# Half of the prompt heads' exponentials turned in 32x32 blocks on VectorE

## The chip, the cores and the metric

The kernel runs on one core of a Trainium2 chip. Its engines are TensorE (PE), VectorE (DVE), ScalarE (ACT), GpSimd (POOL) and SyncE (SP), which here issues the DMAs. The metric is the device time of one execution in microseconds; three runs of the kernel before took 2255.1, 2255.21 and 2255.36 us, a median of 2255.21 us.

## The reference

Two layers of an encoder trunk over two groups of tokens: a prompt of 1024 positions and a sample of 256. Each layer adds to x the normalised output projection of four gated branches (attention, a Fourier mix, spatial gating, attention into memory). The change is in the attention branch: eight query heads of 64, two key/value heads (heads 0 to 3 read key/value head 0, heads 4 to 7 read 1), no mask.

```python
def self_attention(q, k, v):
    ...
    def one_block(qblk):
        s = jnp.einsum('bqkgd,bskd->bkgqs', qblk, k, preferred_element_type=jnp.float32) * scale
        p = jax.nn.softmax(s, axis=-1)
        return jnp.einsum('bkgqs,bskd->bqkgd', p.astype(v.dtype), v)
...
    o_att = self_attention(q, k, v) * jax.nn.silu(ag)
```

All of it is float32. The kernel writes many operands as a sum of a high and a low part in the type f32r, and multiplies the parts.

## The kernel before

The work of a layer comes in the order spatial gating, Fourier, memory attention, the attention's projections, attention, output projection. Attention goes over ten tiles of 128 queries, t = 0 to 7 of the prompt (1024 keys) and 8, 9 of the sample (256 keys); tile by tile over eight heads h; kv = h // 4 is the key/value head and j = h % 4 the place within it.

For one head of a prompt tile: `score` (L742) makes 128 x 1024 scores in PSUM with four matmuls of 512 columns (L752), DVE takes the negated row maximum (L755), ACT the exponential with its row sum (L757). `turn` (L760) transposes the 128 x 1024 exponentials on PE, eight blocks of 128 x 128 (L770), through two PSUM buffers; ACT copies the first half to SBUF (L773), DVE the second (L775). The copies are `pt[kv]`, keys on partitions. `values` (L788) takes one block of 128 keys (kt) at a time for all four heads of each kv: two matmuls of 512 columns onto the two halves of PSUM's partitions (L796); after the last block DVE multiplies by the gate (L801) and SP stores four pieces (L803).

`norm_gate` (L777) turns the reciprocal row sums: a reciprocal (L780) and a broadcast to 128 x 512 (L782) on DVE, four transposes on PE (L785), a product into the gate on DVE (L786). `prep_q` (L713) loads a tile's queries and splits them: high part on ACT (L143), low part on DVE (L144). `turn_q` (L720) transposes them on PE (L724) and copies on ACT (L726) and DVE (L728).

The main loop (L815) sets the order on PE: in the step of head h come the scores of the next head, then one piece of `todo` (the norm and values of the tile before), at h = 4 and 5 a `turn_q` for the next tile, then the turn of h. The block is emitted under `manual_schedule` for PE, so PE runs in this order; on the other engines a scheduler that simulates the timeline decides the order when the program is built. Every engine works through its own list in order. In tile 0 the loop also emits one attention gate (`attention_gates`, L620) every second head, and in tiles 8 and 9 one output product a head (`product`, L871).

## Time and profile before

| | |
|---|---|
| runs | 2255.1, 2255.21, 2255.36 us |
| profiled execution, span from first to last instruction | 2254.6 us |
| PE busy | 2208.9 us, 98% |
| DVE busy | 1167.4 us, 52% |
| ACT busy | 844.2 us, 37% |
| POOL busy | 206.3 us, 9% |
| mean granted TensorE clock | 0.996 |

The profiled execution took its span of 2254.6 us, 0.6 us under the median of the runs. Attention's tiles lie at about 727 to 975 us in layer 0 and 1791 to 2040 us in layer 1. Busy shares are means over the whole span; a group of instructions by line shows its busy time, the mean of one and what the engine waited for before it. A timeline gives start and duration; where like instructions follow each other they are one row with a count, and rows of PE overlap, as matmuls are pipelined. A step is the distance between two starts.

### The profile page before, as it was taken

What the parts mean: (1) busy time and instruction counts of PE and PEld (TensorE: products, weight loads), DVE (VectorE), ACT (ScalarE), POOL (GpSimd) and SP (SyncE); (2) the same over time, 40 slices, a digit from 0 to 9 for tenths busy, and PEclk for the clock granted to TensorE, in tenths of its full rate; (3) what the DMA queues carried; (4) which work ended last, traced back from release to release, by engine and by line L of the source; (5) the groups of instructions that cost most, each with busy time, mean ns of one, the idle gap of its engine ahead of it and who ended that gap; (6) DMA issues with size and microseconds to landing.
All of it is one profiled execution on the core that took longest, in us unless ns stands there. A gap on an engine that the chain in (4) does not pass through costs nothing.

```text
span 2254.6 us, 32607 instructions
## 1 busy us (share of the span) xinstructions
PE 2208.9 (98%) x12872; PEld 1837.5 (82%) x12872; DVE 1167.4 (52%) x2096; ACT 844.2 (37%) x1915; POOL 206.3 (9%) x376
## 2 busy tenths in 40 slices
PE   7999999999999999999999999999999999999997
PEld 7898988888998655578888988888899865567885
DVE  5345344545573777634465344445467377753445
ACT  6133332334332655541254222234342255554121
POOL 2010000000140000000062000000014000000005
PEclk9999999999999999999999999999999999999998
DMA  4123321201122210222343121020112221123234
GB/s 171 59 96 132 128 93 59 99 31 55 58 76 75 66 34 29 84 80 92 112 142 109 57 75 59 33 99 31 59 54 81 78 64 29 31 83 99 88 109 140
DMA packets 96200, 177.31 MB, mean 79 GB/s; under 512 B 12208, under 2 KB 47408, under 8 KB 96048
## 3 DMA queue, kind: packets, MB, share of 16 engines
q1 hardware_dynamic: 96048, 175.23, 23.1%
q8 instruction: 101, 1.65, 0.3%
q14 instruction: 51, 0.42, 0.1%
HBM read 129.05 MB, written 46.14 MB: 78 GB/s over the span
## 4 chain that ended last, share of the span: by engine, by line
PE 90%; ACT 2%; DMA 2%; DVE 2%; POOL 2%; issue 1%; SPq 0%; DVEq 0%; POOLq 0%; ACTq 0%
PE mm L248 34%; PE mm L877 16%; PE mm L261 12%; PE mm L796 6%; PE mm L770 6%; PE s L752 5%; PE mm L311 2%; PE mm L327 1%; PE s L422 1%; PE s L408 1%; PE s L576 1%; PE mm L609 1%; POOL c L902 1%; PE s L217 1%; DMA wr<-in_w_in_dram 1%
## 5 line engine op out<-in xcount | busy, mean ns | idle before, releaser
L248 PE MATMUL mm<-a,ws 128*128 128x512 f32 (+1 forms) x4032 | 795.4, 355 | 0.0
L248 PEld LDWEIGHTS mm<-a,ws 128*128 128x128 f32 x4032 | 663.9, 189 | 102.3 <-issue 0.5
L877 PE MATMUL mm<-ws,a 128*128 128x512 f32 x1632 | 380.5, 391 | 0.0
L877 PEld LDWEIGHTS mm<-ws,a 128*128 128x128 f32 x1632 | 303.9, 188 | 63.7 <-issue 1.6
L261 PE MATMUL mm<-ws,a 128*128 128x256 f32 x2400 | 302.7, 287 | 0.0
L261 PEld LDWEIGHTS mm<-ws,a 128*128 128x128 f32 x2400 | 295.6, 194 | 0.5 <-DVE a L234 0.2
L757 ACT ACTIVATE c<-s,st 128x1024 f32<-128x1024 f32 (+1 forms) x160 | 158.1, 988 | 154.8 <-DVE st L755 153.9
L755 DVE TENSOR_REDUCE st<-s 128x1 f32<-128x1024 f32 (+1 forms) x160 | 170.2, 1064 | 73.1 <-PE s L752 71.0
L770 PEld LDWEIGHTS mm<-ident,c 128*128 128x128 f32 x1088 | 117.1, 141 | 90.1 <-issue 26.0
L273 ACT ACTIVATE c<-mm 128x512 f32<-128x512 f32 (+1 forms) x96 | 50.7, 528 | 342.1 <-PE mm L248 338.3
L274 DVE SCALAR_TENSOR_TENSOR c<-c,mm 128x512 f32<-128x512 f32 (+1 forms) x96 | 57.3, 597 | 231.3 <-ACT c L273 231.3
L752 PE MATMUL s<-c,c 128*128 128x512 f32 (+1 forms) x576 | 162.6, 399 | 1.1 <-ACT c L726 1.1
L770 PE MATMUL mm<-ident,c 128*128 128x128 f32 x1088 | 151.8, 279 | 5.0 <-ACT c L757 5.0
L796 PE MATMUL mm<-a,c 128*64 128x512 f32 x512 | 140.2, 618 | 2.7 <-ACT a L773 2.7
L902 POOL TENSOR_TENSOR c<-c,c 128x512 f32<-128x512 f32 x40 | 56.1, 1401 | 891.5 <-ACT c L897 891.4
L166 ACT ACTIVATE ws<-wr,pre_g 128x256 fp32r<-128x256 f32 x304 | 126.6, 505 | 22.6 <-DMA wr<-in_w_in_dram 16.5
L167 DVE SCALAR_TENSOR_TENSOR ws<-wr,pre_g,ws 128x256 fp32r<-128x256 f32 x304 | 128.7, 484 | 2.2 <-ACT ws L166 2.0
L886 DVE TENSOR_TENSOR c<-c,mm 128x512 f32<-128x512 f32 x120 | 81.1, 682 | 85.1 <-PE mm L877 85.1
L775 DVE COPY a<-mm 128x512 f32<-128x512 f32 x128 | 88.3, 690 | 66.3 <-PE mm L770 66.1
L752 PEld LDWEIGHTS s<-c,c 128*128 128x128 f32 x576 | 98.5, 189 | 14.9 <-ACT c L726 1.3
L150 POOL TENSOR_TENSOR st<-st,mhalf 128x1 f32<-128x1 f32 (+3 forms) x120 | 99.7, 831 | 9.9
L148 POOL TENSOR_SCALAR st<-st 128x1 f32<-128x1 f32 (+3 forms) x120 | 27.2, 227 | 744.2 <-DVE st L654 455.5
(119 smaller groups left out, 2133.9 us busy)
## 6 DMA issues: line engine op xcount, KB each, us to landing
wr<-in_w_in_dram SPq DMA_DIRECT2D x76, 512.0 KB, 4.0
wr<-in_w_out_dram SPq DMA_DIRECT2D x32, 512.0 KB, 4.5
wr<-o SPq DMA_DIRECT2D x64, 256.0 KB, 2.9
c<-in_x_prompt_dram SPq DMA_DIRECT2D x16, 512.0 KB, 6.1
o<-c SPq DMA_DIRECT2D x32, 256.0 KB, 2.0
wr<-in_w_mem_kv_dram SPq DMA_DIRECT2D x16, 512.0 KB, 4.4
q<-c SPq DMA_DIRECT2D x40, 128.0 KB, 1.7
ag<-c SPq DMA_DIRECT2D x80, 64.0 KB, 1.6
```

Of the source, the lines that this page charges most:

```text
L150: nc.gpsimd.tensor_tensor(r, m, mhalf[:, :n], ALU.pow)
L166: nc.scalar.activation(w[:, 0, kk], raw[:, k], AF.Copy, scale=g)
L167: nc.vector.scalar_tensor_tensor(w[:, 1, kk], raw[:, k], g, fv(w)[:, 0, kk], ALU.mult, ALU.subtract)
L248: nc.tensor.matmul(acc[:, :n], w[:, a, k, c * P:(c + 1) * P], hT.t[g][b][:, k, :], start=i == 0, stop=i == 3 * KC - 1)
L261: nc.tensor.matmul(acc[:, :256], hT.t[g][a][:, k, tt * P:(tt + 1) * P], w[:, b, k, :], start=i == 0, stop=i == 3 * KC - 1)
L752: nc.tensor.matmul(s[:, c0:c0 + n], e["qT"][:, h, :], kT[kg][b][:, kv, :], start=b == 0, stop=b == 1)
L755: nc.vector.tensor_reduce(nm, s[:, :nk], axis=AX.X, op=ALU.max, negate=True)
L757: nc.scalar.activation(p[:, :nk], s[:, :nk], AF.Exp, bias=nm, accum_out=e["rs"][:, j, kv:kv + 1])
L770: nc.tensor.transpose(pt[:, kk, :], p[:, c0:c0 + P], ident)
L775: nc.vector.tensor_copy(dst, pt[:, :kn])
L796: nc.tensor.matmul(acc[kv * HD:(kv + 1) * HD].rearrange("p j t -> p (j t)"), vt, e["pt"][kv][:, kt].rearrange("p j t -> p (j t)"), start=k ...
L877: nc.tensor.matmul(acc, oT[g][c][:, a, tt * P:(tt + 1) * P], w[:, b, c, :], start=j == 0, stop=j == 11)
```

## The change

For the heads with j of 2 or 3 in prompt tiles, the turn leaves PE. DVE turns the exponentials in blocks of 32 x 32 within each 32 partitions (L778 of the new kernel) into a buffer `blocks`, and after j = 3 SP issues 16 DMAs (L784), each of 32 partitions by 2 KB, which put block (a, b) into the place (b, a) of a buffer `pd`. So there are 32 such DMAs a tile. Heads with j of 0 and 1 stay on PE; both of their copies are now on ACT (L798). The heads of a prompt tile come in the order 2, 0, 3, 1, 6, 4, 7, 5.

`values` now works on two parts, j of 0 and 1 from `pt` and j of 2 and 3 from `pd`; a matmul has 256 columns instead of 512, and a piece of `todo` has two blocks of keys (L831). The columns of the second part are read in runs of 32. The broadcast of the reciprocals goes to POOL (L805), and `norm_gate` is one step later than before. The query split is on ACT (L726) and POOL (L727), the raw queries are loaded one tile earlier, and both query copies are on ACT (L734). The attention gates keep their number and size but change their order, so that those within tile 0 are of 512 columns. Comments and docstrings elsewhere are removed.

```diff
     def attention_gates(l, hT, ag):
         w = {}
-        for i, g in ((0, 0), (0, 1), (1, 0), (1, 1), (0, 2), (1, 2)):
+        for i, g in ((0, 0), (1, 0), (0, 2), (1, 2), (0, 1), (1, 1)):
...
     def attention(l, q_d, kT, v8, v2, ag, o_d):
+        raw = {}
+        def load_q(t):
+            if t < NT:
+                raw[t] = c2([P, 8, HD])
+                nc.sync.dma_start(raw[t], q_d[t])
         def prep_q(t):
-            q = c2([P, 8, HD])
-            nc.sync.dma_start(q, q_d[t])
+            q = raw.pop(t)
             qhl = c4([P, 8, 2, HD], F32R)
-            split(qhl[:, :, 0, :], qhl[:, :, 1, :], q)
+            nc.scalar.copy(qhl[:, :, 0, :], q)
+            nc.gpsimd.tensor_tensor(qhl[:, :, 1, :], q, fv(qhl)[:, :, 0, :], ALU.subtract)
             return qhl
-        def turn_q(qhl, qT, kvs):
-            for kv in kvs:
-                pt = mm([P, 4, P], F32R)
-                for j in range(4):
-                    nc.tensor.transpose(pt[:, j, :], qhl[:, 4 * kv + j].rearrange("p a d -> p (a d)"), ident_r)
-                if kv == 0:
-                    nc.scalar.copy(qT[:, 0:4], fv(pt))
-                else:
-                    nc.vector.tensor_copy(qT[:, 4:8], fv(pt))
+        def turn_q(qhl, qT, kv):
+            pt = mm([P, 4, P], F32R)
+            for j in range(4):
+                nc.tensor.transpose(pt[:, j, :], qhl[:, 4 * kv + j].rearrange("p a d -> p (a d)"), ident_r)
+            nc.scalar.copy(qT[:, 4 * kv:4 * kv + 4], fv(pt))
         tiles = {}
         def open_tile(t):
-            g, _ = group_of(t)
-            nk = SEQ if g < 2 else DEC
-            gt = c2([P, 4, P])
-            nc.sync.dma_start(gt, ag[t])
-            alloc = a16 if g < 2 else c4
-            tiles[t].update(
-                nk=nk, gt=gt, rs=st([P, 4, 2], tag="rowsum", bufs=3),
-                pt=[alloc([P, nk // P, 4, P], F32) for _ in range(2)])
+            e = dict(prompt=t < 8, nk=SEQ if t < 8 else DEC, qT=c4([P, 8, P], F32R),
+                     rs=st([P, 4, 2], tag="rowsum", bufs=3))
+            tiles[t] = e
+        def open_rest(t):
+            e = tiles[t]
+            e["gt"] = c2([P, 4, P])
+            nc.sync.dma_start(e["gt"], ag[t])
+            if e["prompt"]:
+                e["pt"] = a16([P, 8, 2, 2, P], F32)
+                e["pd"] = a16([P, 4, 2, 8, 2, 32], F32)
+            else:
+                e["pt"] = [c4([P, 2, 4, P]) for _ in range(2)]
         def score(t, h):
             g, _ = group_of(t)
@@ -759,87 +770,121 @@
         def turn(t, h):
             e = tiles[t]
-            nkt = e["nk"] // P
             kv, j = h // 4, h % 4
             p = e.pop(h)
-            for half in range((nkt + 3) // 4):
-                kn = min(4, nkt)
+            if e["prompt"] and j >= 2:
+                if j == 2:
+                    e["blocks"] = a8([P, 4, 8, 2, 32], F32)
+                nc.vector.transpose(e["blocks"][:, :, :, j - 2].rearrange("p b k q -> p k b q"),
+                                    p.rearrange("p (k b q) -> p k b q", b=4, q=32))
+                if j == 3:
+                    for r in range(4):
+                        for a in range(4):
+                            b = (a + r) % 4
+                            nc.sync.dma_start(
+                                e["pd"][32 * b:32 * b + 32, a, kv].rearrange("p k j q -> p (k j q)"),
+                                e["blocks"][32 * a:32 * a + 32, b].rearrange("p k j q -> p (k j q)"))
+                return
+            for half in range(2 if e["prompt"] else 1):
+                kn = 4 if e["prompt"] else 2
                 pt = mm([P, 4, P])
                 for kk in range(kn):
                     c0 = (half * 4 + kk) * P
                     nc.tensor.transpose(pt[:, kk, :], p[:, c0:c0 + P], ident)
-                dst = e["pt"][kv][:, half * 4:half * 4 + kn, j, :]
-                if half == 0:
-                    nc.scalar.copy(dst, pt[:, :kn])
+                if e["prompt"]:
+                    dst = e["pt"][:, half * 4:half * 4 + kn, kv, j, :]
                 else:
-                    nc.vector.tensor_copy(dst, pt[:, :kn])
-
-        def norm_gate(t):
+                    dst = e["pt"][kv][:, :, j, :]
+                nc.scalar.copy(dst, pt[:, :kn])
+        def norm_rows(t):
             e = tiles[t]
             r = st([P, 4, 2], tag="rowsum_r", bufs=2)
             nc.vector.reciprocal(r, e["rs"])
-            rb = c2([P, 4, 2, HD])
-            nc.vector.tensor_copy(rb, r.unsqueeze(3).to_broadcast([P, 4, 2, HD]))
+            e["rb"] = c2([P, 4, 2, HD])
+            nc.gpsimd.tensor_copy(e["rb"], r.unsqueeze(3).to_broadcast([P, 4, 2, HD]))
+        def norm_gate(t):
+            e = tiles[t]
             rt = mm([P, 4, P])
             for j in range(4):
-                nc.tensor.transpose(rt[:, j, :], rb[:, j].rearrange("p a d -> p (a d)"), ident)
+                nc.tensor.transpose(rt[:, j, :], e["rb"][:, j].rearrange("p a d -> p (a d)"), ident)
             nc.vector.tensor_tensor(e["gt"], e["gt"], rt, ALU.mult)
-        def values(t, kt):
+        def values(t, part, kts):
             e = tiles[t]
-            nkt = e["nk"] // P
-            if kt == 0:
+            if "acc" not in e:
                 e["acc"] = mm([P, 4, P])
             acc = e["acc"]
-            for kv in range(2):
-                vt = (v8 if t < 8 else v2)[:, kt, kv * HD:(kv + 1) * HD]
-                nc.tensor.matmul(acc[kv * HD:(kv + 1) * HD].rearrange("p j t -> p (j t)"), vt,
-                                 e["pt"][kv][:, kt].rearrange("p j t -> p (j t)"),
-                                 start=kt == 0, stop=kt == nkt - 1)
-            if kt == nkt - 1:
-                o = c2([P, 4, P])
-                nc.vector.tensor_tensor(o, acc, e["gt"], ALU.mult)
-                for j in range(4):
-                    nc.sync.dma_start(o_d[j][:, t * P:(t + 1) * P], o[:, j, :])
-                del tiles[t]
-
+            last = e["nk"] // P - 1
+            for kt in kts:
+                for kv in range(2):
+                    out = acc[kv * HD:(kv + 1) * HD]
+                    vt = (v8 if t < 8 else v2)[:, kt, kv * HD:(kv + 1) * HD]
+                    if not e["prompt"]:
+                        out, src = out.rearrange("p j t -> p (j t)"), e["pt"][kv][:, kt].rearrange("p j t -> p (j t)")
+                    elif part == 0:
+                        out, src = out[:, 0:2].rearrange("p j t -> p (j t)"), e["pt"][:, kt, kv].rearrange("p j t -> p (j t)")
+                    else:
+                        out = out[:, 2:4].rearrange("p j (a q) -> p j a q", q=32)
+                        src = e["pd"][:, :, kv, kt].rearrange("p a j q -> p j a q")
+                    nc.tensor.matmul(out, vt, src, start=kt == 0, stop=kt == last)
+        def finish(t):
+            e = tiles.pop(t)
+            o = c2([P, 4, P])
+            nc.vector.tensor_tensor(o, e["acc"], e["gt"], ALU.mult)
+            for j in range(4):
+                nc.sync.dma_start(o_d[j][:, t * P:(t + 1) * P], o[:, j, :])
+        load_q(0)
+        load_q(1)
         qhl = prep_q(0)
         yield
-        tiles[0] = dict(qT=c4([P, 8, P], F32R))
-        turn_q(qhl, tiles[0]["qT"], (0, 1))
         open_tile(0)
-        score(0, 0)
+        for kv in range(2):
+            turn_q(qhl, tiles[0]["qT"], kv)
+        open_rest(0)
+        order = {True: (2, 0, 3, 1, 6, 4, 7, 5), False: tuple(range(8))}
+        work = [(t, i, h) for t in range(NT) for i, h in enumerate(order[t < 8])]
+        score(0, work[0][2])
         yield
-        work = [(t, h) for t in range(NT) for h in range(8)]
         todo = []
-        for i, (t, h) in enumerate(work):
-            if h == 2 and t + 1 < NT:
+        for n, (t, i, h) in enumerate(work):
+            if i == 2 and t + 1 < NT:
                 qhl = prep_q(t + 1)
-            if h == 4 and t + 1 < NT:
-                tiles[t + 1] = dict(qT=c4([P, 8, P], F32R))
+            if i == 4 and t + 1 < NT:
+                load_q(t + 2)
                 open_tile(t + 1)
-            if i + 1 < len(work):
-                score(*work[i + 1])
+            if i == 7 and t + 1 < NT:
+                open_rest(t + 1)
+            if n + 1 < len(work):
+                score(work[n + 1][0], work[n + 1][2])
             if todo:
-                todo.pop(0)()
-            if h in (4, 5) and t + 1 < NT:
-                turn_q(qhl, tiles[t + 1]["qT"], (h - 4,))
+                for f in todo.pop(0):
+                    f()
+            if i in (4, 5) and t + 1 < NT:
+                turn_q(qhl, tiles[t + 1]["qT"], i - 4)
             turn(t, h)
-            if h == 7:
-                for f in todo:
-                    f()
-                todo = [lambda t=t: norm_gate(t)]
-                nkt = tiles[t]["nk"] // P
-                todo += [lambda t=t, kt=kt: values(t, kt) for kt in range(nkt)]
-                if nkt == 8:
-                    a, b = todo[0], todo[1]
-                    todo[0:2] = [lambda a=a, b=b: (a(), b())]
-            yield t, h
-        for f in todo:
-            f()
+            if i == 7:
+                for fs in todo:
+                    for f in fs:
+                        f()
+                norm_rows(t)
+                if t < 8:
+                    todo = [[lambda t=t, part=part, k=k: values(t, part, (k, k + 1))]
+                            for part in range(2) for k in range(0, 8, 2)]
+                    todo[1].append(lambda t=t: norm_gate(t))
+                else:
+                    todo = [[lambda t=t: norm_gate(t)]] + [[lambda t=t, k=k: values(t, 0, (k,))] for k in range(2)]
+                todo[-1].append(lambda t=t: finish(t))
+            yield t, i
+        for fs in todo:
+            for f in fs:
+                f()
```

PE, at the boundary of tiles 1 and 2 of layer 0: `s2_` are scores, `mm_` PSUM results, `a16_` the turned exponentials. Before, the steps of the first head of tile 2:

```order
L770 MATMUL mm_1039_7618<-ident_61,c4_1032_7585 128x128 x4
L770 MATMUL mm_1040_7624<-ident_61,c4_1032_7585 128x128 x4
L752 MATMUL s2_1041_7630<-c4_693_5346,c4_1013_7514 128x512
L752 MATMUL s2_1041_7630<-c4_694_5347,c4_1013_7514 128x512
L752 MATMUL s2_1041_7630<-c4_695_5348,c4_1013_7514 128x512
L752 MATMUL s2_1041_7630<-c4_696_5349,c4_1013_7514 128x512
L785 MATMUL mm_1046_7643<-ident_61,c2_1045_7641 128x128 x4
L796 MATMUL mm_1047_7649<-a16_961_7278,c4_698_5351 64x512
L796 MATMUL mm_1047_7649<-a16_962_7279,c4_698_5351 64x512
L770 MATMUL mm_1048_7652<-ident_61,c4_1037_7608 128x128 x4
L770 MATMUL mm_1049_7658<-ident_61,c4_1037_7608 128x128 x4
```

After, the second of tile 2's steps and the end of the first:

```order
L763 MATMUL s2_1032_7632<-c4_695_5348,c4_1005_7509 128x512
L763 MATMUL s2_1032_7632<-c4_696_5349,c4_1005_7509 128x512
L831 MATMUL mm_1035_7641<-a16_975_7375,c4_698_5351 64x256 x4
L763 MATMUL s2_1037_7648<-c4_693_5346,c4_1005_7509 128x512
L763 MATMUL s2_1037_7648<-c4_694_5347,c4_1005_7509 128x512
L763 MATMUL s2_1037_7648<-c4_695_5348,c4_1005_7509 128x512
L763 MATMUL s2_1037_7648<-c4_696_5349,c4_1005_7509 128x512
L831 MATMUL mm_1035_7641<-a16_975_7375,c4_698_5351 64x256 x4
L811 MATMUL mm_1040_7661<-ident_61,c2_1031_7630 128x128 x4
L793 MATMUL mm_1041_7667<-ident_61,c4_1034_7639 128x128 x4
L793 MATMUL mm_1042_7673<-ident_61,c4_1034_7639 128x128 x4
```

Before, every step has S (L752), V (L796) and T (L770). Now the step of head 2 has S and V only; the step of head 0 has S (here of head 3), V, N (L811) and T.

POOL in attention of layer 0. Before, its list goes from the key and query norms straight to the output's products (L902):

```order
L150 TENSOR_TENSOR st_890_6718<-st_889_6716,mhalf_65 128x4
L148 TENSOR_SCALAR st_894_6755<-st_893_6753 128x4
L150 TENSOR_TENSOR st_895_6757<-st_894_6755,mhalf_65 128x4
L902 TENSOR_TENSOR c4_1386_9063<-c4_1386_9063,c4_1580_10330 128x512
L902 TENSOR_TENSOR c4_1392_9091<-c4_1392_9091,c4_1580_10330 128x512
```

After, the low parts of the queries (L727, `c4_` of the tile) and the broadcasts (L805) stand in between; `c4_1043` are the queries of tile 3, `c2_1031` the broadcast for tile 1, and N above (`mm_1040`) reads `c2_1031`:

```order
L805 COPY c2_983_7400<-st_982_7398 128x512
L727 TENSOR_TENSOR c4_995_7449<-c2_955_7267,c4_995_7449 128x8x64
L727 TENSOR_TENSOR c4_1043_7679<-c2_1004_7507,c4_1043_7679 128x8x64
L805 COPY c2_1031_7630<-st_1030_7628 128x512
L805 COPY c2_1079_7860<-st_1078_7858 128x512
L727 TENSOR_TENSOR c4_1091_7909<-c2_1052_7737,c4_1091_7909 128x8x64
L727 TENSOR_TENSOR c4_1139_8139<-c2_1100_7967,c4_1139_8139 128x8x64
L805 COPY c2_1127_8090<-st_1126_8088 128x512
```

The broadcast for tile 1 stands behind the low part of tile 3's queries, which needs their high part. ACT makes that one (`c4_1043`, L726); its list after, in tile 2, `c4_1034` and `c4_1039` being the exponentials of heads 0 and 3:

```order
L798 COPY a16_975_7375<-mm_1028_7616 128x4x128
L798 COPY a16_975_7375<-mm_1029_7622 128x4x128
L768 ACTIVATE c4_1034_7639,st_1006_7510<-s2_1032_7632,st_1033_7637 128x1024
L768 ACTIVATE c4_1039_7655,st_1006_7510<-s2_1037_7648,st_1038_7653 128x1024
L726 CAST c4_1043_7679<-c2_1004_7507 128x8x64
L798 COPY a16_1022_7595<-mm_1041_7667 128x4x128
L798 COPY a16_1022_7595<-mm_1042_7673 128x4x128
```

The cast stands behind both exponentials. In the POOL list the same order returns two tiles on: L805, L805, L727, L727.

DVE in tile 2 of layer 0, after: `c4_1026`, `c4_1039` and `c4_1049` are the exponentials of heads 2, 3 and 6.

```order
L766 TENSOR_REDUCE st_1019_7568<-s2_1018_7563 128x1
L766 TENSOR_REDUCE st_1025_7602<-s2_1024_7597 128x1
L803 RECIPROCAL st_1030_7628<-st_957_7270 128x8
L766 TENSOR_REDUCE st_1033_7637<-s2_1032_7632 128x1
L778 STREAM_TRANSPOSE a8_1036_7646<-c4_1026_7604 128x8x4x32
L766 TENSOR_REDUCE st_1038_7653<-s2_1037_7648 128x1
L778 STREAM_TRANSPOSE a8_1036_7646<-c4_1039_7655 128x8x4x32
L836 TENSOR_TENSOR c2_1027_7610<-mm_987_7411,c2_925_7076 128x512
L812 TENSOR_TENSOR c2_974_7373<-c2_974_7373,mm_1040_7661 128x512
L766 TENSOR_REDUCE st_1045_7687<-s2_1044_7682 128x1
L766 TENSOR_REDUCE st_1048_7717<-s2_1047_7712 128x1
```

Before, a copy out of PSUM (L775) stood behind each reduce; now a transpose (L778) a pair of heads stands there, and the broadcast (L782) is gone. The product of tile 0 (L836) stands behind the transpose of head 3.

## Rows read from the trace of the kernel before

**Rows 1.** The page's busy shares; waits of PE: us, times, longest.

```profile
PE 2208.9 (98%) x12872; PEld 1837.5 (82%) x12872; DVE 1167.4 (52%) x2096; ACT 844.2 (37%) x1915; POOL 206.3 (9%) x376
...
PE mm L770 <- ACT c L757: 5.0, 8, 1.2
PE mm L796 <- ACT a L773: 2.7, 2, 1.4
```

**Rows 2.** Windows of two prompt tiles: span, engines' busy times, PEclk, DMA share, GB/s.

```profile
760.00:784.80 24.80, 24.80 (x142) 14.77 (x140) 18.15 (x23) 14.45 (x26) 0.00 (x0) 1.00 0.09 27
784.80:809.60 24.80, 24.80 (x142) 14.77 (x140) 18.15 (x23) 14.45 (x26) 0.00 (x0) 1.00 0.12 33
```

**Rows 3.** Timeline of PE in layer 0: start, duration, engine, line, operation.

```profile
811.12 1.17 PE L752 MATMUL s<-c,c 128*128 128x512 f32 x4
812.23 1.08 PE L796 MATMUL mm<-a,c 128*64 128x512 f32 x4
813.24 1.09 PE L770 MATMUL mm<-ident,c 128*128 128x128 f32 x8
814.08 1.17 PE L752 MATMUL s<-c,c 128*128 128x512 f32 x4
...
812.71 0.60 PE L796 MATMUL mm<-a,c 128*64 128x512 f32 x2
...
808.73 0.60 PE L785 MATMUL mm<-ident,c 128*128 128x128 f32 x4
809.26 0.65 PE L796 MATMUL mm<-a,c 128*64 128x512 f32 x2
...
822.12 0.54 PE L724 MATMUL mm<-ident_r,c 128*128 128x128 f32 x4
822.49 0.30 PE L770 MATMUL mm<-ident,c 128*128 128x128 f32 x1
```

**Rows 4.** Groups by line and shape: count, busy time, mean ns of one.

```profile
L902 POOL TENSOR_TENSOR c<-c,c 128x512 f32<-128x512 f32 x40 | 56.1, 1401 | 891.5 <-ACT c L897 891.4
L143 ACT CAST c<-c 128x512 fp32r<-128x512 f32 x28 | 17.5, 624 | 4.0 <-DVE c L491 4.0
L144 DVE TENSOR_TENSOR c<-c,c 128x512 fp32r<-128x512 f32 x28 | 19.1, 684 | 3.5 <-ACT c L143 3.5
L782 DVE COPY c<-st 128x512 f32<-128x512 f32 x20 | 8.4, 420 | 0.1
L726 ACT CAST c<-mm 128x512 fp32r<-128x512 f32 x20 | 11.6, 578 | 0.9 <-PE mm L724 0.9
L775 DVE COPY a<-mm 128x512 f32<-128x512 f32 x128 | 88.3, 690 | 66.3 <-PE mm L770 66.1
L773 ACT COPY a<-mm 128x512 f32<-128x512 f32 x128 | 74.2, 580 | 9.9 <-PE mm L770 9.9
```

**Rows 5.** Timeline of DVE and ACT there, and of a turn that waited.

```profile
812.33 1.22 DVE L755 TENSOR_REDUCE st<-s 128x1 f32<-128x1024 f32 x1 [0.24 <-PE s L752]
...
813.65 1.11 ACT L757 ACTIVATE c<-s,st 128x1024 f32<-128x1024 f32 x1 [1.72 <-DVE st L755]
814.76 0.58 ACT L773 COPY a<-mm 128x512 f32<-128x512 f32 x1
...
755.99 1.12 ACT L757 ACTIVATE c<-s,st 128x1024 f32<-128x1024 f32 x1
757.25 0.55 PE L770 MATMUL mm<-ident,c 128*128 128x128 f32 x3 [0.42 <-ACT c L757]
```

**Rows 6.** Timeline of PE: longest waits in tile 0 and sample tiles.

```profile
739.91 0.33 PE L770 MATMUL mm<-ident,c 128*128 128x128 f32 x1 [1.22 <-ACT c L757]
...
934.55 0.64 PE L796 MATMUL mm<-a,c 128*64 128x512 f32 x1 [1.36 <-ACT a L773]
```

**Rows 7.** SP's four stores of a tile; landing of one: KB, us.

```profile
882.26 1.75 SPq L803 DMA_DIRECT2D o<-c  x4
...
o<-c SPq DMA_DIRECT2D x80, 64.0 KB, 1.6
```

## The prediction

> **What bounds the kernel now.** I read the busy shares first: TensorE (PE) is busy for 98% of the span and next to nothing else is long [rows 1]. The waits of PE then say which of its rare gaps lie in attention: two lines there, 5.0 us before the turns (L770) and 2.7 us before the values (L796), over both layers [rows 1]. So attention is bound by what PE has to do, and the table by windows shows it: a prompt tile takes 24.80 us, all of it PE, with VectorE (DVE) at 18.15 us, ScalarE (ACT) at 14.45 us, GpSimd (POOL) at nothing and the clock at 1.00 [rows 2]. Last comes the timeline of one head. Its PE steps, start to start, are 1.11 us for scores (S), 1.01 us for values (V), 0.84 us for the eight turns (T): 2.96 us [rows 3]. A quarter turn of the queries (Q) adds 822.49 - 822.12 = 0.37 us, the norm's turn (N) 809.26 - 808.73 = 0.53 us [rows 3]. Per tile: 8 x 2.96 + 2 x 0.37 + 0.53 = 24.95 us, near the window's 24.80.
>
> **What goes.** In each of 16 prompt tiles (eight in each of two layers) four heads lose their turn on PE: 64 x 0.84 = -53.8 us.
>
> **What the split of the values adds.** V keeps its columns but cuts each matmul from 512 to 256. A V is now two pairs of passes (four records), and a pair takes 812.71 - 812.23 = 0.48 us [rows 3]. The same 512 columns of fp32 cost in T half of 0.84 = 0.42 us, so some 0.06 us of a pair does not scale with the columns. With four half pairs instead of two pairs, V grows by between 0 (it scales fully) and 2 x 0.06 = 0.12 us. I take 0.11 (the row's remainder, a little less for rounding): 128 x 0.11 = +14.1 us. The Trainium skill (TensorEngine Tiling (Array Packing), Instruction Overhead) puts some 60 cycles on a matmul, 0.025 us at 2.4 GHz as an estimate; by it the V term would be 128 x 0.05 = 6.4 instead of 14.1 us. The row shows more per pair, and I go by the row. PE's work so falls by 39.7 us, and a tile to about 22.4 us.
>
> **Does the chain through the DVE transpose keep up?** No row shows this instruction. The bounds for a block transpose of 128x1024 are 0.84 us (twice the 128x512 copy within SBUF, L782 [rows 4]) and 2.44 us (two passes at the rate of a 1024-element reduce, 1.22 us [rows 5]). I take one pass, 1.22 us, as for the reduce, which also touches every element once. In a pair of heads a (on DVE) and b (on PE), DVE runs reduce a, transpose a, reduce b in that order (only in the first pair of a tile reduce b comes ahead of transpose a). From the start of S(a): the reduce starts after 812.33 - 811.12 = 1.21, the exponential 1.32 later, at 2.53 [rows 3, 5]; a turn may follow an exponential's start after 757.25 - 755.99 = 1.26 [rows 5], at 3.79; the transpose holds DVE for 1.22, to 5.01; reduce b to exponential b 1.32, and 1.26 more: T(b) is possible at 7.59. PE gets there after three S, three V and one T: 3 x 1.11 + 3 x 1.12 + 0.84 = 7.53. It is a tie, so each tenth of a microsecond that the transpose takes beyond 1.22 shows; a wait at T(b) delays the next S(a) less than the next T(b), since that S was already issued, and I count half the excess. Where two query casts stand on ACT before the exponential of head 7, the tie breaks: S(7) at u; Q1 ends at u + 1.11 + 1.12 + 0.37 = 2.60, the cast [rows 4] holds ACT to about 3.2, transpose 7 starts 1.26 later at 4.46 and ends at 5.68, exponential 5 starts at 7.00, T(5) is possible at u + 8.26. PE has S, V, Q, T, S, V, S, V before it: 3 x 1.11 + 3 x 1.12 + 0.37 + 0.84 = 7.90. I take 0.35 in each of 16 tiles: +5.6 us.
>
> **The step that I think eats the gain: POOL's queue.** The broadcast of the reciprocal row sums (RB, L805) and the low half of the queries (lo, L727) are both on POOL now, and POOL works in order. For tiles 2, 4 and 6 the queue has the lo of the *next* tile ahead of the RB of the *previous* one. That lo needs the high half, which ACT casts (L726) behind the exponential of head 3; N, which needs RB, stands on PE at the second head of that tile, just behind S(3) and V. From the start of S(3): exponential 3 starts at 2.53, ACT is free 1.11 later (814.76 - 813.65) [rows 5], the cast takes 0.62, lo as a POOL tensor_tensor of 128x512 1.40 [rows 4]. RB has no row on POOL: between 0.42 (the copy on DVE that it replaces) and 1.40 (POOL's tensor_tensor), I take 0.9, the middle, as nothing says which row is nearer. Sum 2.53 + 1.11 + 0.62 + 1.40 + 0.90 = 6.56. PE arrives at 1.11 + 1.12 = 2.23. PE so waits 4.3 us, three times in each layer: 6 x 4.3 = +26.0 us. Bounds: lo at DVE's 0.68 [rows 4] and RB at 0.42 give 3.1 x 6 = 19; both at 1.40 give 4.8 x 6 = 29. Behind the waiting N on PE stand T(0) and all later scores. DVE's product of tile t-2 (L836), which stands behind transpose 3 in the same tiles, would end at 3.79 + 1.22 + 0.68 = 5.7 after S(3), under that wait; if the wait were gone, it would be next, since a turn's PSUM buffer waits for it.
>
> **The rest.** Moved to other engines at no cost: both copies of a turn on ACT (two of 0.58 a head on PE instead of one, 14.45 us of a 22.4 us tile busy before); lo and RB leave DVE 1.1 us a tile. The DMAs: 32 of 64 KB a tile, 512 in all. Four stores hold SP for 1.75 us, 0.44 each, and 64 KB land after 1.6 us [rows 7]; 16 x 0.44 + 1.6 = 8.6 us, while the last group (transpose 7, at u + 5.6) is wanted by the V of the next tile's fifth head, about u + 21: 15 us of room. SP's other work in that time, four stores, a gate and a query load, is about 2.5 us. So 0; they show only if a block takes twice that. The DMA share of 0.09 to 0.12 [rows 2] leaves room. Start of attention: lo on POOL 1.40 instead of 0.68 on DVE before the first Q, 2 x 0.7 = +1.4. The waits of tile 0 and the first sample head (1.22 and 1.36 in layer 0 [rows 6], with their like 7.7 in all [rows 1]) stay about as they are, between 0 and -7.7: -2. In tile 8, three products of the output (L877 before) may wait for conversions that ACT has in order behind the late loads: between 0 and +9: +3. The gates only change places: three of 512 columns stand in tile 0 instead of three of 256, and the sum of PE's work is the same: 0.
>
> **Sum.** -53.8 + 14.1 + 26.0 + 5.6 + 1.4 - 2 + 3 = -5.7 us on a span of 2254.6. The median of 2255.21 is 0.6 above the span, so 2249.5 us. I say 2249. A difference below about 0.2% (4.5 us) can't be told from none here.
>
> **Rivals.**
> *The cheap end.* The transpose runs at the rate of the copy within SBUF (0.84) and the half-width passes scale fully. For it: 0.42 for 512 elements is a DVE row [rows 4]. Against: 0.69 for a copy from PSUM and 0.68 for lo [rows 4] on the same size. V loses its 14.1 and the T(5) wait its 5.6: 2249.5 - 19.7 = 2230 us, the queue on POOL being what is left.
> *The transpose takes two passes (slower).* At 2.44 us it is 1.22 over the tie, in each of the 64 pairs of heads; half of it, 0.61 x 64 = 39, makes 2288 us. It decides the sign from an excess of about 0.18 on (5.7 / 32), that is from 1.4 us. For it: DVE's time is the one price here without any row, and it has no cover. Against: the reduce of 1024 elements takes one pass [rows 5]. The Trainium skill (VectorE: DVE Perf Modes, The three transpose paths) gives 311 ns for 128x128 bf16 on VectorE; eight of these are 2.49 us as an estimate, and by it the time would be this rival's. No run shows yet whether that figure holds for one long instruction.
> *The strided operand.* The moved half is read by PE in pieces of 32 elements. At half rate for these, 16 half pairs a tile cost 0.21 more each: 3.4 x 16 = 54, less the 5.6 of waits that it hides: 2298 us. Against: nothing but that no row has such an operand.
>
> **Chances.** The forecast 0.53, the cheap end 0.17, two passes 0.20, the strided operand 0.07, something else (late blocks) 0.03. Around the forecast its own bounds (POOL 19 to 29, V 0 to 14, edges -10 to +9, a transpose up to 1.5 us) make 2233 to 2262; of its 0.53, 0.31 lie below 2250.7, 0.15 within 4.5 us and 0.07 above 2259.7. With the cheap end: faster 0.48; same 0.16; slower 0.36 with the two others. The range for 8 in 10 reaches from the cheap end to the two passes: 2228 to 2288.
>
> **What would show it.** Right: N (L811) waits 3 to 5 us on POOL in tiles 2, 4 and 6 of each layer, six times, and not in tiles 1, 3, 5; V at 1.12 us; STREAM_TRANSPOSE near 1.2 us; odd prompt tiles at 22.4 to 23 us, even ones near 27. Wrong: no wait at L811 (then RB is quick or the cast early); waits of ACT's exponentials before T(b) in every pair (a slow transpose); V parts that differ in duration (the stride); V waiting for DMA.

## The result and the profile after

The changed kernel takes 2266.14 us (median of four runs, 2264.89 to 2270.51), the kernel before 2255.28 in the same session: a ratio of 1.0052 (95% interval 1.0037 to 1.0066). It is slower, by about 11 us. The forecast was 2249 us, 6 us faster. The profiled execution's span is 2264.1 us against 2254.6.

The page after, its line of busy shares, answers to [rows 1]:

```profile
PE 2176.4 (96%) x12872; PEld 1834.0 (81%) x12872; DVE 1124.0 (50%) x1972; ACT 854.2 (38%) x1935; POOL 241.3 (11%) x416
```

PE is busy for 32.5 us less in a span that is 9.5 us longer. So PE now waits, and the waits of PE after say where (line waited at, releaser, total us, times, longest):

```profile
PE mm L811 <- POOL c L805: 24.3, 6, 4.1
...
PE mm L922 <- ACT c L798: 9.5, 4, 3.0
PE mm L793 <- ACT c L768: 6.8, 15, 0.5
PE mm L922 <- ACT c L929: 6.5, 3, 3.4
...
PE mm L831 <- DMA a<-a: 1.5, 2, 0.9
```

The first row is the wait that the prediction put on POOL's queue, with its size and count. The rows of L922, 16.0 us, are new: L922 is the output's product (L877 before), and before it never waited for another engine. The next rows show the new operations by line and shape (count, then busy us and mean ns):

```profile
L778 DVE STREAM_TRANSPOSE a<-c 128x1024 f32<-128x1024 f32 x64 | 79.6, 1243 | 56.9 <-ACT c L768 51.5 <-DMA a<-a 2.9 <-DMA c<-q 2.5
...
L727 POOL TENSOR_TENSOR c<-c,c 128x512 fp32r<-128x512 f32 x20 | 25.5, 1273 | 312.8 <-ACT c L726 250.3 <-DMA a<-a 62.5
...
L805 POOL COPY c<-st 128x512 f32<-128x512 f32 x20 | 12.2, 612 | 280.2 <-DVE st L803 239.3 <-PE mm L793 40.9
```

The transpose takes one pass, 1.24 us, against 1.22 taken. The timeline of PE after one of the six waits, in tile 2 of layer 0, answers to [rows 3]:

```profile
783.35 1.11 PE L811 MATMUL mm<-ident,c 128*128 128x128 f32 x4 [4.12 <-POOL c L805]
784.26 1.91 PE L793 MATMUL mm<-ident,c 128*128 128x128 f32 x8
785.83 1.55 PE L763 MATMUL s<-c,c 128*128 128x512 f32 x4
787.30 1.08 PE L831 MATMUL mm<-a,c 128*64 128x256 f32 x8
788.32 1.20 PE L763 MATMUL s<-c,c 128*128 128x512 f32 x4
```

Two things are to be seen. V's step is 788.32 - 787.30 = 1.02 us against 1.01 before: four half pairs cost what two pairs cost. And right behind the wait, T's step is 785.83 - 784.26 = 1.57 us instead of 0.84, and S's 1.47 instead of 1.11. The windows say why (start and end, length, busy us of PE, PEld, DVE, ACT and POOL, PEclk, DMA share):

```profile
780.00:783.00 3.00, 0.00 (x0) 0.00 (x0) 1.82 (x2) 1.41 (x3) 1.52 (x2) 1.00 0.45 104
783.00:786.50 3.50, 3.15 (x14) 3.05 (x15) 0.69 (x1) 0.88 (x2) 0.30 (x1) 0.53 0.53 105
786.50:790.00 3.50, 3.50 (x22) 1.96 (x22) 1.68 (x2) 1.50 (x3) 0.00 (x0) 0.98 0.86 251
```

PE stood idle for 4.12 us, and then the granted clock was near half, the lower of its two levels (1.2 GHz), for about 3 us. By the steps of PE from N to the second S behind it (4.97 us here; at the higher level of the clock 0.53 + 0.84 + 1.11 + 1.01 = 3.49) the three waits of layer 0 lost a further 1.5, 1.5 and 2.7 us in this way, those of layer 1 2.8, 1.2 and 1.5: 11.1 us in all.

By stages the balance is this. The first product of the output starts at 935.75 us before and 927.15 after in layer 0: up to there 8.6 us are won. The eleventh starts at 979.41 before and 984.47 after. So the stretch of the sample tiles between them grew from 43.7 to 57.3 us. In layer 1 the same stretch grew from 43.7 to 53.8 (1999.36 to 2053.20), with 5.7 us won ahead of it. In all, 14.3 us won in the prompt tiles and 23.8 lost in the sample tiles: 9.5, the difference of the spans. The rows of layer 0, two of the kernel before and two after (the last one is cut off by the window):

```profile
935.75 3.00 PE L877 MATMUL mm<-ws,a 128*128 128x512 f32 x12
...
979.41 3.00 PE L877 MATMUL mm<-ws,a 128*128 128x512 f32 x12
```

```profile
927.15 3.00 PE L922 MATMUL mm<-ws,a 128*128 128x512 f32 x12
...
984.47 0.71 PE L922 MATMUL mm<-ws,a 128*128 128x512 f32 x2
```

What the sample tiles wait for is seen on SP. Its timeline at the end of the prompt tiles of layer 0 (start, time for the group, queue, line):

```profile
913.45 10.01 SPq L784 DMA_DIRECT2D a<-a  x16
923.50 0.58 SPq L721 DMA_DIRECT2D c<-q  x1
924.18 10.66 SPq L784 DMA_DIRECT2D a<-a  x16
934.89 0.58 SPq L746 DMA_DIRECT2D c<-ag  x1
935.57 0.41 SPq L906 DMA_DIRECT2D wr<-o  x1
```

Sixteen blocks' DMAs (L784) hold SP for 10.0 us, 0.63 each, where I had taken 0.44 from the stores [rows 7]. A tile's 32 are 20.2 us; with 1.98 for the stores and 0.58 for each of two loads SP needs up to 23.3 us a tile. PE takes 22.1 us a tile where no such DMA is in its way (nodma below). So SP is now the longer of the two by its work alone. In this run it doesn't fall further and further behind, as PE's waits stretch a tile to 24.9 us (two tiles between the rows of L811 at 783.35 and 833.21), and SP still waits six times for a transpose:

```profile
SPq L784 <- DVE a L778: 8.0, 6, 2.5
```

What counts at the end of the prompt tiles is its order: the loads of the output's operand (L906) stand behind the last sixteen blocks (10.66 us) and go out from 935.57 on, 8.4 us after the first product. Before, they went out 2.2 us ahead of it:

```profile
933.58 3.80 SPq L861 DMA_DIRECT2D wr<-o  x6
```

ACT then waits in front of their conversion, with the sample's copy queued behind, and PE behind that. ACT's timeline:

```profile
938.62 0.63 ACT L909 ACTIVATE a<-wr 128x512 fp32r<-128x512 f32 x1 [7.12 <-DMA wr<-o]
```

and PE's, where the product behind the wait takes 4.61 us instead of 3.00, again at the lower clock (first row). Not every such wait has this behind it: in layer 1 the product behind one of 2.95 us took 3.02 (second row).

```profile
939.56 4.61 PE L922 MATMUL mm<-ws,a 128*128 128x512 f32 x12 [2.99 <-ACT c L798]
...
2026.89 3.02 PE L922 MATMUL mm<-ws,a 128*128 128x512 f32 x12 [2.95 <-ACT c L929]
```

### The profile page after: what moved, and what is told of

It reads as the page before. It is cut to its first block, busy times and chain, and to the rows that moved or that the text cites. A ratio compares the mean times of both kernels' runs of the same rounds, so it can differ in the third digit from the quotient of the medians.

```text
span 2264.1 us, 33322 instructions
## 1 busy us (share of the span) xinstructions
PE 2176.4 (96%) x12872; PEld 1834.0 (81%) x12872; DVE 1124.0 (50%) x1972; ACT 854.2 (38%) x1935; POOL 241.3 (11%) x416
## 4 chain that ended last, share of the span: by engine, by line
PE 81%; SPq 7%; DMA 3%; DVE 3%; issue 2%; ACT 2%; POOL 1%; DVEq 0%; POOLq 0%; ACTq 0%
PE mm L248 33%; PE mm L922 16%; PE mm L261 12%; SPq L784 6%; PE s L763 3%; PE mm L831 3%; PE mm L327 2%; PE mm L311 2%; PE mm L793 2%; PE s L422 1%; PE s L408 1%; PE s L576 1%; PE mm L609 1%; PE s L217 1%; PE s L366 1%
## 5 line engine op out<-in xcount | busy, mean ns | idle before, releaser
L922 PE MATMUL mm<-ws,a 128*128 128x512 f32 x1632 | 385.3, 395 | 16.0 <-ACT c L798 9.5
L922 PEld LDWEIGHTS mm<-ws,a 128*128 128x128 f32 x1632 | 307.1, 190 | 82.6 <-ACT c L798 10.5
L763 PE MATMUL s<-c,c 128*128 128x512 f32 (+1 forms) x576 | 167.4, 409 | 2.6 <-ACT c L768 1.9
L274 DVE SCALAR_TENSOR_TENSOR c<-c,mm 128x512 f32<-128x512 f32 (+1 forms) x96 | 57.3, 596 | 217.9 <-ACT c L273 217.9
L831 PE MATMUL mm<-a,c 128*64 128x256 f32 x1024 | 143.7, 397 | 1.8 <-DMA a<-a 1.5
L831 PEld LDWEIGHTS mm<-a,c 128*64 128x64 f32 x1024 | 63.9, 138 | 66.3 <-issue 43.0
L778 DVE STREAM_TRANSPOSE a<-c 128x1024 f32<-128x1024 f32 x64 | 79.6, 1243 | 56.9 <-ACT c L768 51.5
L793 PE MATMUL mm<-ident,c 128*128 128x128 f32 x576 | 85.7, 287 | 7.0 <-ACT c L768 6.8
L144 DVE TENSOR_TENSOR ws<-wr,ws 128x1024 fp32r<-128x1024 f32 x48 | 56.8, 1221 | 65.0 <-ACT ws L143 65.0
```

Source lines behind the costliest of these rows:

```text
L763: nc.tensor.matmul(s[:, c0:c0 + n], e["qT"][:, h, :], kT[kg][b][:, kv, :], start=b == 0, stop=b == 1)
L793: nc.tensor.transpose(pt[:, kk, :], p[:, c0:c0 + P], ident)
L831: nc.tensor.matmul(out, vt, src, start=kt == 0, stop=kt == last)
L922: nc.tensor.matmul(acc, oT[g][c][:, a, tt * P:(tt + 1) * P], w[:, b, c, :], start=j == 0, stop=j == 11)
```

## The experiments

The theory after the result: SP, at 0.63 us a block DMA, is over its time, and both losses follow from that. The sample tiles lose 24 us because loads stand behind blocks in its queue; and POOL's bad order is the builder's answer to a late SP in its own timeline. The low clock behind the waits adds to both. Rivals: ACT, with more copies, is late by itself; the transfers, not SP, are the cost; the clock has nothing to do with the waits.

**POOL in the order of the code (mp).**

```diff
-        with tc.manual_schedule(engines={mybir.EngineType.PE}):
+        with tc.manual_schedule(engines={mybir.EngineType.PE, mybir.EngineType.Pool}):
```

> The changed kernel with POOL, too, in the order in which the code issues its work, so that the broadcast for tile t stands ahead of the low part of tile t+2's queries. If the wait at L811 came from POOL's queue, it goes (24.3 us, 6 waits); next late is DVE's product L836 behind the transpose of head 3, worth about 2.5 us before the turn's second half, so 9 us of waits are won, and up to 9 more if the low clock behind those waits goes with them: 2248 to 2257 us. Rival (SP is full: 32 DMAs of 0.63 and 3.1 for the rest make 23.3 us a tile): the time comes back as waits of the values on the blocks' DMAs, 2260 or more.

Measured: 2261.57 us, ratio to before 1.0029 (1.0017 to 1.004), against 1.0052 (1.0037 to 1.0066) of the changed kernel: some 5 us won, with intervals that just meet. That is above the 2248 to 2257 us expected. It is the rival's time, but not the rival's sign: the values wait 1.8 us for the blocks, after 1.5 in the changed kernel. The waits at L811 are gone, and what the prediction named as next late is there, at the size worked out (2.5 us, six times):

```profile
PE mm L793 <- DVE c L836: 14.1, 6, 2.6
```

So POOL's order was the cause of the wait at L811, but not the only late thing in those tiles: DVE's product stands behind the transpose of head 3. The sample stretch stays long (57.7 and 56.4 us between the same two products). In layer 0, the timeline of PE has the three waits for L836 so:

```profile
785.08 0.66 PE L793 MATMUL mm<-ident,c 128*128 128x128 f32 x4 [2.55 <-DVE c L836]
...
830.40 0.66 PE L793 MATMUL mm<-ident,c 128*128 128x128 f32 x4 [1.30 <-ACT c L768]
833.38 1.11 PE L793 MATMUL mm<-ident,c 128*128 128x128 f32 x4 [2.33 <-DVE c L836]
...
882.63 0.80 PE L793 MATMUL mm<-ident,c 128*128 128x128 f32 x4 [2.43 <-DVE c L836]
```

and the windows over them (columns as above):

```profile
780.00:790.00 10.00, 7.45 (x49) 4.33 (x48) 6.65 (x7) 4.90 (x9) 1.26 (x1) 1.00 0.50 122
...
830.00:840.00 10.00, 7.27 (x30) 4.42 (x32) 4.28 (x6) 4.26 (x9) 1.27 (x1) 0.66 0.58 151
...
880.00:890.00 10.00, 7.57 (x39) 4.66 (x38) 4.87 (x5) 4.22 (x8) 1.27 (x1) 0.83 0.60 150
```

The clock stays at 1.00 behind the wait of 2.55 us. It falls where two waits lie 3 us apart, and also behind a single one of 2.43 us. So its loss comes with the waits, but the length of a wait doesn't tell whether it comes.

**The output's first loads on ACT's queue (ldact).**

```diff
-                        nc.sync.dma_start(raw[:, cc, :], o_d[4 * qt + c + cc][:, t0:t0 + n])
+                        (nc.scalar if qt == 2 else nc.sync).dma_start(raw[:, cc, :], o_d[4 * qt + c + cc][:, t0:t0 + n])
```

> The changed kernel with the loads of the first output operand (L906, qt of 2) issued by ACT instead of SP. If the sample tiles lose their 24 us (13.7 in layer 0, 10.2 in layer 1) because these loads stand behind the blocks' DMAs on SP, the products' waits (16 us) and the low clock behind them go: 2242 us or a little more. Rival (ACT itself is late, with both copies of every turn and the query casts): the waits of L922 stay and the time stays at 2266.

Measured: 2260.56 us, ratio 1.0023 (1.0013 to 1.0032); the sample stretch is 50.7 and 50.9 us instead of 57.3 and 53.8. The conversions of these loads (L909) now wait 0.31 us at most in layer 0, where one waited 7.12, so the first part of the theory holds. Less came than expected, since another load stands in the same queue: the output's weights (L159) are issued by SP from 940.6 us on, behind the blocks, and ACT waits for them instead:

```profile
944.18 1.04 ACT L143 CAST ws<-wr 128x1024 fp32r<-128x1024 f32 x1 [7.39 <-DMA wr<-in_w_out_dram]
```

So neither ACT's own work nor the one load explains the loss. What the loads share is that they stand behind the blocks in SP's queue.

**Both (mpld).** The two edits above together.

> Both edits together: POOL in the order of the code, first output loads on ACT. If the two costs are independent: 2224 to 2233 us. If SP is full, the values wait for the blocks' DMAs and less comes of it.

Measured: 2249.32 us, ratio 0.9974 (0.9963 to 0.9985): 6 us faster than before, but 16 short of the expectation. The waits for L836 (14.5 us) and the weights behind the blocks remain.

**No blocks' DMAs (nodma).** Left out: the blocks never reach pd, so the values of half the prompt heads are missing.

```diff
+        pd1 = a16([P, 4, 2, 8, 2, 32], F32)
+        nc.gpsimd.memset(pd1, 0.0)
...
-                e["pd"] = a16([P, 4, 2, 8, 2, 32], F32)
+                e["pd"] = pd1
...
-                    for r in range(4):
...
+                    pass
```

> The changed kernel without the blocks' DMAs: one buffer pd per layer, filled once, so that the values of heads with j of 2 and 3 are left out of the output. The builder then also puts POOL's broadcasts in alternating order. Theory (SP's queue, POOL's queue, and the clock that falls behind each wait): 2266 - 24 in the sample tiles - 24 of L811 - 10 of clock = 2208 us. Rival (the DMAs cost nothing, ACT is late): 2232 us, with the sample tiles' waits left.

Measured: 2212.13 us, ratio 0.9804 (0.9789 to 0.9818). The waits at the norm's turn and of the output's products are gone, the clock is 0.997, the sample stretch is 44.1 us in both layers. The largest wait left in attention is the small one at the turns; the values wait 3.6 us for ACT's copies.

```profile
PE mm L790 <- ACT c L770: 8.6, 18, 0.7
```

A prompt tile takes PE 22.10 us, from one turn of the norm (L811 of the changed kernel) to the next:

```profile
802.92 0.66 PE L808 MATMUL mm<-ident,c 128*128 128x128 f32 x4
...
825.02 0.66 PE L808 MATMUL mm<-ident,c 128*128 128x128 f32 x4
```

So 54 us hang on these 512 DMAs, not on ACT's work and not on the chain through the transpose. Part of them comes by way of the builder: POOL's list alternates here too.

**Half of the blocks' DMAs on ACT's queue (alt), and POOL's work back on DVE (altdve).**

```diff
-                            nc.sync.dma_start(
+                            (nc.scalar if r % 2 else nc.sync).dma_start(
```

> The changed kernel with every second group of blocks' DMAs (r of 1 and 3) issued by ACT, so SP has 16 a tile instead of 32: 10 us of 23.3 fall away there. The builder then also puts POOL's broadcasts and DVE's product L836 in alternating order. Theory (full SP queue behind both losses): no wait at L811, the sample tiles as before, 2212 to 2220 us, near the run without DMAs. Rival (the transfers themselves, not SP's issue of them, are the cost: DMA share, SBUF, landing): the values and the output's loads still wait, above 2235 us; or ACT, whose queue now waits for transposes, delays exponentials: above 2235 too, with waits at the turns.

Measured: 2299.29 us, ratio 1.0191 (1.0169 to 1.0212): the second rival came true, ACT delays the exponentials. POOL's order is the alternating one and the waits at L811 are gone, but ACT's list now holds 256 DMAs, which hold ACT as they hold SP, some 0.6 us each, and the exponentials stand behind them. One such place, and the waits of ACT:

```profile
801.40 2.53 ACTq L784 DMA_DIRECT2D a<-a  x4
804.03 1.11 ACT L768 ACTIVATE c<-s,st 128x1024 f32<-128x1024 f32 x1 [2.70 <-DMA a<-a]
```

```profile
ACT c L768 <- DMA a<-a: 93.4, 29, 6.2
```

and those of PE:

```profile
PE mm L831 <- ACT a L798: 37.8, 16, 5.3
```

The run settles one thing all the same. All 512 transfers are still there, and both losses of the changed kernel are gone: no wait at L811, no wait of the output's products, a sample stretch of 44.6 and 45.3 us. So the same transfers bring neither loss when SP issues half of them. The kernel is slower here, which gives them more room; dbl below keeps the bytes and doubles the DMAs.

The second of the pair has besides:

```diff
-            nc.gpsimd.tensor_tensor(qhl[:, :, 1, :], q, fv(qhl)[:, :, 0, :], ALU.subtract)
+            nc.vector.tensor_tensor(qhl[:, :, 1, :], q, fv(qhl)[:, :, 0, :], ALU.subtract)
...
-            nc.gpsimd.tensor_copy(e["rb"], r.unsqueeze(3).to_broadcast([P, 4, 2, HD]))
+            nc.vector.tensor_copy(e["rb"], r.unsqueeze(3).to_broadcast([P, 4, 2, HD]))
```

> As with the DMAs on two queues, and the broadcast and the low part of the queries back on DVE. If moving them to POOL was needed for the gain, DVE's extra 1.1 us a tile delays reduces and transposes, 64 pairs at a tie: 5 to 20 us above the run with two queues. If not: the same within 4 us, or 1.5 us faster at the attention's start (0.7 a layer).

Measured: 2298.26 us, ratio 1.0188 (1.0164 to 1.0211), the same as alt. With ACT's queue in the way of both this doesn't tell whether the move to POOL was needed; that stays open.

**Prompt tile 7 turned on PE (t7).**

```diff
-            if e["prompt"] and j >= 2:
+            if t < 7 and j >= 2:
...
-                    dst = e["pt"][:, half * 4:half * 4 + kn, kv, j, :]
+                    dst = e["pt" if j < 2 else "pd"][:, half * 4:half * 4 + kn, kv, j % 2, :]
```

> The changed kernel with prompt tile 7 (the last before the sample tiles) turned on PE as before, so that SP has no blocks' DMAs just ahead of the output's loads; POOL's order stays. Theory: the 24 us of the sample tiles go, PE works 4 x 0.84 more in each layer (7 us), the waits at L811 stay (24 us): about 2249 us. Rival (the sample tiles are late for another reason, such as ACT's conversions): 2273 us.

Measured: 2260.55 us, ratio 1.0021 (1.0012 to 1.003). The sample stretch is 44.1 us in both layers, every wait of the output's products is gone, and the six waits at L811 stay (24.3 us, as before the edit).

So the loss of the sample tiles did come from the blocks just ahead of the loads. The total is 12 us above the expectation: from the first query turn to the first product it now takes 220.9 us instead of 213.2 and 212.8 in the two layers. Of these 7.7 and 8.1 us, 3.4 are PE's work in each layer. ACT's copies (L798) hold the values of tile 7 for 1.5 and 1.8 us more and one turn for 0.5, the blocks' DMAs hold values in tile 0 for 0.4 and 1.3 more, and by the steps of PE the lower clock behind the waits at L811 takes 7.5 and 6.7 us where it took 5.7 and 5.5.

**The diagonal blocks copied by POOL (diag), and tile 7 on PE besides (diagt7).** For r = 0 a block stays on its partitions, so it needs no DMA.

```diff
-                            nc.sync.dma_start(
+                            (nc.gpsimd.tensor_copy if r == 0 else nc.sync.dma_start)(
```

> The changed kernel with the four blocks of each group that stay on their partitions (r of 0) copied by POOL, so that SP has 24 blocks' DMAs a tile instead of 32: 24 x 0.63 + 3.1 = 18.2 us a tile instead of 23.3, against PE's 22.4. The builder then alternates POOL's broadcasts with the low parts and puts DVE's product L836 ahead of the transposes. Theory (SP over its time is behind both losses): no waits at L811 or for L836, and less of the sample tiles' loss, as 7.6 instead of 10 us of DMAs stand ahead of the output's loads: 2220 us, at most 2232. Rival (any DMA within SBUF costs, or POOL's copies hold back the broadcast): waits at L811 or before the values, above 2240.

Measured: 2224.73 us, ratio 0.9869 (0.9854 to 0.9883), as expected: one line away from the changed kernel, and 29 us faster than the kernel before. The largest wait of PE in attention:

```profile
PE s L763 <- ACT c L768: 12.5, 4, 4.9
```

No wait at L811, none for L836, none of the output's products; the sample stretch is 44.1 us. POOL's list alternates, broadcast (L805), low part (L727), broadcast:

```profile
795.25 0.61 POOL L805 COPY c<-st 128x512 f32<-128x512 f32 x1 [0.45 <-DVE st L803]
801.96 1.28 POOL L727 TENSOR_TENSOR c<-c,c 128x512 fp32r<-128x512 f32 x1 [6.09 <-DMA o<-c]
```

This order comes with fewer DMAs on SP: it is there in nodma and alt as well, though nothing in these edits tells POOL so. SP has 15.1 us of blocks' DMAs a tile left (24 of 0.63), and waits 37.8 us for transposes where it waited 8.0 in the changed kernel:

```profile
SPq L784 <- DVE a L778: 37.8, 12, 4.3
```

SP's own list changed too, which the expectation had not foreseen. The loads of the output's operand now stand ahead of the last twelve blocks:

```profile
894.40 7.48 SPq L784 DMA_DIRECT2D a<-a  x12
901.98 7.69 SPq L906 DMA_DIRECT2D wr<-o  x6
910.60 8.09 SPq L784 DMA_DIRECT2D a<-a  x12
```

So the sample tiles lose nothing here because the order is another one as well, not only because fewer DMAs stand in it. A rest of the loss lies in tile 7 instead: a conversion (L909) waits 4.12 us for its load, exponentials stand behind it on ACT, and PE waits 4.75 of the 12.5 us above.

> As with POOL's copies, and prompt tile 7 turned on PE. PE works 7 us more, the sample tiles have nothing ahead of their loads. If some 12 us or more of the sample tiles' loss were left in the run with POOL's copies, this is the faster one: 2215 to 2220; if they were gone, it is 4 to 7 us slower than that run.

Measured: 2222.64 us, ratio 0.9862 (0.9845 to 0.9878), not to be told from diag: the 7 us more of PE's work are paid by exponentials of tile 7 that no longer wait (the 12.5 us above are 2.8 here). These two are the fastest complete kernels of the study.

**Each block's DMA in two halves (dbl).** With POOL's copies, as in diag.

```diff
-                            (nc.gpsimd.tensor_copy if r == 0 else nc.sync.dma_start)(
-                                e["pd"][32 * b:32 * b + 32, a, kv].rearrange("p k j q -> p (k j q)"),
-                                e["blocks"][32 * a:32 * a + 32, b].rearrange("p k j q -> p (k j q)"))
+                            if r == 0:
+                                nc.gpsimd.tensor_copy(dst, src)
+                            else:
+                                for c in (0, 256):
+                                    nc.sync.dma_start(dst[:, c:c + 256], src[:, c:c + 256])
```

> The kernel with POOL's copies, and each of the 24 blocks' DMAs of a tile as two of half the bytes (32 partitions by 1 KB). If SP's 0.63 us is a price of each DMA, 48 of them take 30 us and with the rest 33 us a tile, 11 over PE: 2225 + 16 x 11 = about 2400 us, values waiting for DMAs. If it is a price of the bytes, 48 take 15 us and the time stays within 5 us of 2225.

Measured, one run: 2395.89 us. The same bytes in twice as many DMAs cost 171 us over diag. SP still needs 0.63 us for each (here 24 in 15.08 us):

```profile
822.85 15.08 SPq L790 DMA_DIRECT2D a<-a  x24
```

So the price on SP is one of each DMA, not of its bytes. The time came out as expected (about 2400), but not where it was expected: the values wait only 14.4 us for the blocks. SP waits 0.3 us in all for a transpose now; the transposes wait 102.8 us for SP's DMAs, and PE behind them 53.5 us for exponentials at the turns. And POOL's list is back in the order of the changed kernel, low part ahead of the broadcast, with 56.6 us of waits of PE for it:

```profile
825.80 1.26 POOL L727 TENSOR_TENSOR c<-c,c 128x512 fp32r<-128x512 f32 x1 [11.17 <-ACT c L726]
827.01 0.61 POOL L809 COPY c<-st 128x512 f32<-128x512 f32 x1
```

POOL's own work is the same in diag and dbl; only the number of SP's DMAs differs. So POOL's order hangs on SP's load. Why the builder's timeline answers it in this way is not shown.

## Why the prediction was wrong

The sign was wrong, the range (2228 to 2288) held the time. Step by step:

- *What goes, and the chain through the transpose*: right. One pass of 1.24 us, no wait in the plain pairs, 0.48 us before T(5) in most tiles (6.8 us in all, 5.6 predicted).
- *POOL's queue*: right in place, count and size, 24.3 us against 26.0. RB was 0.61 us and lo 1.27, below the values taken. The product L836 as the next late was right too (mp: 14.1 us). What I did not see is why POOL had this order: I took it as given, and it hung on SP (diag and dbl).
- *The split of the values*: wrong by some 13 us to the other side. V's step is 1.02 us, against 1.01 before and 1.12 predicted. The 0.06 us that a pair of passes took beyond the columns does not come with each pair. The 60 cycles of the Trainium skill (TensorEngine Tiling (Array Packing), Instruction Overhead), by which 6.4 us were worked out, don't show here either.
- *The rest, "So 0" for the DMAs*: this is the step that failed. I took 0.44 us from a group of stores for a DMA of another kind, which took 0.63, and I compared one group of 16 with its own deadline (8.6 against 15 us) instead of adding up what SP has to do in a tile: up to 23.3 us, against 22.1 of PE. With 0.44 the sum would have been 17, and no alarm; a resource without a row needed a bound from both sides, as the transpose had one, and a sum by tile. The cost came out not at the blocks' readers (1.5 us at L831) but at what stands behind them in SP's queue: the sample tiles lost 23.8 us, where 3 were forecast and 9 were the bound. t7 and nodma show it from two sides; without the 512 DMAs the kernel takes 54 us less.
- *The clock*: not in the sum. Each 4 us wait of PE at L811 was followed by 2.4 to 5.5 us at the lower level (twice what its steps lost), 5.7 us of loss in layer 0 and 5.5 in layer 1, and there was more behind some waits in the sample tiles (the product behind a wait of 2.99 us took 4.61 us instead of 3.00).

Of the 15 us between the forecast (-5.7 on the span) and the result (+9.5): V -13, the waits of POOL and T(5) together near 0, the sample tiles +21, the clock behind L811's waits +11; about 3 us the other way are small gains ahead of the sample tiles that I did not follow. That the range held the time is luck in part: V's error and the clock's, each over 10 us, went opposite ways.

## What to carry to other kernels

When a change adds many DMAs, add up the issuing queue's time per stage as for an engine, at the price of the nearest kind and above it, and compare it with the stage; then look at what stands behind them in that queue. A wait of TensorE can cost more than its length, as what follows it can run at the lower clock: 11.1 us on top of 24.3 at L811. And when a builder's order looks odd, ask which late resource its timeline answers: taking eight DMAs a tile off SP changed the order of POOL's, DVE's and SP's own lists, and turned +0.5% into -1.3%.

## What the runs showed of the hardware

- A DMA within SBUF of 32 partitions holds SP for 0.63 us whether a partition's piece is 2 KB or 1 KB (after and dbl); a 64 KB one landed after 2.0 us (median of 512), a 32 KB one after 1.9.
- DMAs issued by ACT can hold its computing instructions for long: 93.4 us of exponentials waiting with 256 of them (alt). With 24 loads on that queue (ldact) this was not seen.
- A block transpose of 128x1024 fp32 on DVE took 1243 ns. The Trainium skill (VectorE: DVE Perf Modes, The three transpose paths) gives 311 ns for 128x128 bf16; eight of these are 2.49 us as an estimate, and the one long instruction takes half of that.
- A matmul that reads its moving operand in runs of 32 columns was as fast as one that reads it in one run: V's step is 1.02 us in part 0 (above) and 1.01 in part 1:

```profile
842.28 1.08 PE L831 MATMUL mm<-a,c 128*64 128x256 f32 x8
843.29 0.54 PE L733 MATMUL mm<-ident_r,c 128*128 128x128 f32 x4
```

- The granted clock fell to its lower level (1.2 GHz) behind single waits of PE of 2.43 us (mp) and 4.0 to 4.1 us (after), and not behind single ones of 2.55 (mp) and 2.95 us (after).
